# Attention weights of the dilated groups: sent through DRAM as rows and loaded back spread over features, with the score and value runs put side by side

## The chip, the cores and the metric

The kernel runs on one core of a Trainium2 chip. The metric is the device time of one execution in microseconds (us). TensorE (PE) multiplies matrices into eight PSUM banks, VectorE (DVE), ScalarE (ACT) and GpSimd (POOL) work elementwise on SBUF and PSUM, SyncE (SP) and also ACT and POOL issue DMA transfers. Each engine works through its own instructions in order and waits on semaphores for the others.

## The reference, cut to what matters

Two layers of a decoder trunk on x of 512 tokens and 1024 features, all float32. Of each layer, the part that the change touches is the dilated attention: 18 heads of 64 features in three groups of six, with (window, dilation) = (128,1), (512,4), (2048,16). For each head position the three groups' outputs are averaged with weights that are a softmax over the groups' log denominators:

```python
for gi, (window, dilation) in enumerate(ATTN_GROUPS):
    o, lse = _dilated_window_attention(q_a[:, :, gi], k_a[:, :, gi], v_a[:, :, gi], ..., window, dilation)
    outs.append(o.astype(jnp.float32))
    lses.append(lse)
wts = jax.nn.softmax(jnp.stack(lses, axis=0), axis=0)
y_a = jnp.sum(wts[..., None] * jnp.stack(outs, axis=0), axis=0)
...
y_r = _retention(q_r, k_r, v_r)                      # 4 heads, rotary, chunkwise
merged = sigmoid(gate_a) * (y_a @ w_attn_proj) + sigmoid(gate_b) * ((silu(g_r) * y_r) @ w_ret_proj)
x = layer_norm(ALPHA * x + merged @ w_out)
x = layer_norm(ALPHA * x + swiglu(x))
```

## The kernel before, in words

Most of the time goes into large projections. A float32 product is made of three matmuls of 32-bit parts, high by high, high by low and low by high (`mm3`, `whi`/`wlo`, `xh`/`xl`, and `xs` for sums of blocks); the weights are loaded by SP and split by ACT (L347) and DVE (L355). All matmuls are issued by `mm` at L96; rows of the profile tell them apart by their tiles: `ps<-...` are projections, `px<-qk` attention scores, `px<-s,v` attention values.

Attention runs beside the projections as a list of small steps. The steps stand in the queue `side`; after each projection step `tick` takes from it at a rate that `pace` sets, so the places of the steps in the list, with `nothing` as filler, set the order on every engine:

```python
def tick(us):
    if side:
        credit[0] += rate[0] * us
        while side and credit[0] >= 1.0:
            credit[0] -= 1.0
            side.popleft()()
```

Per layer there are three pairs of heads (hp 0, 1, 2). Pairs 0 and 1 run beside other query, key and value projections, pair 2 beside the first rotary projection of the retention part. For one pair and each of four tiles i of 128 queries there are three steps. `scores(i)` issues the products of queries and keys into two PSUM tiles; DVE adds the bias and finds the minimum of the negated scores (L542), ACT takes the exponentials with their sums (L545). `turn(i)` transposes the eight (six for tile 0) blocks on PE (L555) and ACT copies them back (L556). `values(i)` multiplies by the values, and ACT copies the result to `y` (L569). The first group is in token order ("order 0"), the two dilated groups share an order by stride ("order 1"), so two weights per token and head are needed.

After the tiles comes the tail. `swap` stores minima and sums of order 1 to DRAM (`exd`, L583), `swapped` loads them in the other order (`mb`, L586), `weigh` makes both weights per token and head on DVE (L592 to L603) and stores those of order 1 to DRAM (`exd2`, L602; the profile shows it as exd too), `weighed` loads them in stride order (`fa`, L608). For each order, `expand` spreads a weight over the 64 features of its head on POOL (`fe`, L615), `turn_weights` transposes four blocks on PE (L621) into PSUM, and `combine` multiplies `y` by them on DVE (L626, L628) and adds order 1 to order 0 (L630). The tail of one pair runs in the list of the next one; the last tail runs beside the rotary projection and the first retention head. ACT issues the stores and loads of the tail in its own queue.

Of the kernel before, what the change touches and what calls it, by code (L numbers as in the profile page):

```python
# [20 lines left out]
P = 128  # L21
# [35 lines left out]
def hybrid_kernel(ctx, tc, x, x_t, w_first, rel_t, b_cols, b_rows, w_in, w_attn_proj, w_ret_proj, w_out,  # L57
# [457 lines left out]

    latest = {}

    def attention_pair(hp, qk, v, yp, bias, yaT):


        y = yp()
        nm = sm.tile([P, 2, NI, 2], F32, tag="nm", name="nm", bufs=2)
        ls = sm.tile([P, 2, NI, 2], F32, tag="ls", name="ls", bufs=2)
        wrk = {}

        def scores(i):
            tk = slice(i * P, (i + 1) * P)
            pxs = [psum() for _ in range(2)]
            j0 = 1 if i == 0 else 0
            prs = [slice(hh * HD, (hh + 1) * HD) for hh in range(2)]  # L530
            for px, pr in zip(pxs, prs):
                mm(px[:, j0 * P:2 * P], qk[0][pr, 0, tk], qk[0][pr, 1, (i - 1 + j0) * P:(i + 1) * P], True, True)
            for j in range(2):
                for px, pr in zip(pxs, prs):
                    mm(px[:, (2 + j) * P:(3 + j) * P], qk[1 + j][pr, 0, tk], qk[1 + j][pr, 1, tk], True, True)
            ss = [wk.tile([P, 2, 2 * P], F32, tag="w2", name="s") for _ in range(2)]
            for hh in range(2):
                for od in range(2):
                    n0 = j0 * P if od == 0 else 0
                    s = ss[od]  # L540
                    m_, l_ = nm[:, od, i, hh:hh + 1], ls[:, od, i, hh:hh + 1]
                    dve.tensor_tensor_reduce(out=s[:, hh, n0:], in0=pxs[hh][:, od * 2 * P + n0:(od + 1) * 2 * P],  # L542
                                             in1=bias[hp][hh][:, od, n0:], scale=-1.0, scalar=3e38,
                                             op0=ALU.add, op1=ALU.min, accum_out=m_)
                    act.activation(out=s[:, hh, n0:], in_=s[:, hh, n0:], func=AF.Exp, bias=m_, scale=-1.0, accum_out=l_)  # L545
            wrk[i] = (pxs, ss, j0)

        def turn(i):
            pxs, ss, j0 = wrk[i]
            for od in range(2):  # L550
                j1 = j0 if od == 0 else 0
                px = pxs[od].rearrange("p (h c) -> p h c", h=2)
                for hh in range(2):
                    for j in range(j1, 2):
                        pe.transpose(px[:, hh, j * P:(j + 1) * P], ss[od][:, hh, j * P:(j + 1) * P], ident)  # L555
                act.copy(out=ss[od][:, :, j1 * P:], in_=px[:, :, j1 * P:])  # L556
            latest["sT"] = ss[1]

        def values(i):
            pxs, sTs, j0 = wrk.pop(i)  # L560
            px = pxs[0]
            for od in range(2):
                j1 = j0 if od == 0 else 0
                vs = (v[i - 1][:, 0] if i else None, v[i][:, 0]) if od == 0 else (v[i][:, 1], v[i][:, 2])
                for j in range(j1, 2):
                    for hh in range(2):
                        cs = slice(hh * HD, (hh + 1) * HD)
                        mm(px[cs, od * P:(od + 1) * P], vs[j][:, cs], sTs[od][:, hh, j * P:(j + 1) * P], j == j1, j == 1)
            act.copy(out=y[:, :, i], in_=px[:, :2 * P].rearrange("p (o t) -> p o t", o=2))  # L569

        fa = sm.tile([P, 2, NI, 2], F32, tag="fa", name="fa", bufs=2)
        mb = sm.tile([P, NI, 4], F32, tag="mb", name="mb", bufs=2)
        wb = sm.tile([P, NI, 2], F32, tag="wb", name="wb", bufs=2)

        exd = drp.tile([S, 4], F32, tag="exd", name="exd", bufs=2)
        exd2 = drp.tile([S, 2], F32, tag="exd2", name="exd2", bufs=2)

        def swap():

            pk = sm.tile([P, NI, 4], F32, tag="pk", name="pk", bufs=2)  # L580
            act.copy(out=pk[:, :, 0:2], in_=nm[:, 1])
            act.copy(out=pk[:, :, 2:4], in_=ls[:, 1])
            act.dma_start(exd.rearrange("(l r) c -> l r c", r=4), pk)  # L583

        def swapped():
            act.dma_start(mb, exd.rearrange("(i p) c -> p i c", p=P))  # L586

        def weigh():
            mn = sm.tile([P, NI, 2], F32, tag="mn", name="mn", bufs=2)
            ea = sm.tile([P, 2, NI, 2], F32, tag="ea", name="ea", bufs=2)  # L590
            wa = sm.tile([P, NI, 2], F32, tag="wa", name="wa", bufs=2)
            dve.tensor_copy(mn, latest["sT"][:, 0, P:P + 2 * NI].rearrange("p (i h) -> p i h", i=NI))  # L592
            dve.tensor_tensor(out=mn, in0=nm[:, 0], in1=mb[:, :, 0:2], op=ALU.min)
            dve.tensor_tensor(out=ea[:, 0], in0=mn, in1=nm[:, 0], op=ALU.subtract)
            dve.tensor_tensor(out=ea[:, 1], in0=mn, in1=mb[:, :, 0:2], op=ALU.subtract)
            act.activation(out=ea, in_=ea, func=AF.Exp)
            dve.tensor_tensor(out=wa, in0=ea[:, 0], in1=ls[:, 0], op=ALU.mult)
            dve.tensor_tensor(out=wb, in0=ea[:, 1], in1=mb[:, :, 2:4], op=ALU.mult)
            dve.tensor_tensor(out=wa, in0=wa, in1=wb, op=ALU.add)
            dve.reciprocal(out=wa, in_=wa)  # L600
            dve.tensor_tensor(out=wb, in0=ea[:, 1], in1=wa, op=ALU.mult)
            act.dma_start(exd2.rearrange("(i p) c -> p i c", p=P), wb)  # L602
            dve.tensor_tensor(out=fa[:, 0], in0=ea[:, 0], in1=wa, op=ALU.mult)  # L603

        def weighed():

            act.copy(out=fa[:, 1], in_=latest["sT"][:, 0, P:P + 2 * NI].rearrange("p (i h) -> p i h", i=NI))
            act.dma_start(fa[:, 1], exd2.rearrange("(l r) c -> l r c", r=4))  # L608

        wide_, weights = {}, {}  # L610

        def expand(od):

            wide_[od] = work("fe")
            pool.tensor_copy(out=wide_[od].rearrange("p (i h e) -> p i h e", i=NI, h=2),  # L615
                             in_=fa[:, od].unsqueeze(3).to_broadcast([P, NI, 2, HD]))

        def turn_weights(od):
            px = weights[od] = psum()
            for i in range(NI):  # L620
                pe.transpose(px[:, i * P:(i + 1) * P], wide_[od][:, i * P:(i + 1) * P], ident)  # L621

        def combine(od):
            yo = y[:, od].rearrange("p i t -> p (i t)")
            if od == 0:
                dve.tensor_tensor(out=yaT[:, hp], in0=yo, in1=weights[od], op=ALU.mult)  # L626
            else:
                dve.tensor_tensor(out=yo, in0=yo, in1=weights[od], op=ALU.mult)  # L628
                yr = yaT[:, hp].rearrange("p (l r) -> p r l", r=4)
                dve.tensor_tensor(out=yr, in0=yr, in1=y[:, od], op=ALU.add)  # L630

        places = [[] for _ in range(30)]
        for i in range(NI):
            for at, f in ((0, scores), (6, turn), (9, values)):
                places[(0, 7, 14, 20)[i] + at].append(lambda f=f, i=i: f(i))
        ops = [f for p_ in places for f in p_ or [nothing]]
        ops.append(swap)
        steps = [[lambda f=f, od=od: f(od) for f in (expand, turn_weights, combine)] for od in range(2)]
        tail = [swapped, weigh] + steps[0] + [weighed] + steps[1]
        return ops, tail  # L640

    VB = 288
# [10 lines left out]
    def layer(ly, cp):  # L653
# [12 lines left out]
        csp = yap  # L666
        cos = csp.tile([P, S], F32, name="cos")
        sin = csp.tile([P, S], F32, name="sin")

        def slot(name="op", dt=F32R):  # L670
            return opp.tile([P, 2, S], dt, tag="op", name=name)
# [62 lines left out]
        with stage("attn") as ap_, stage("attw", 4) as aw:  # L734
# [212 lines left out]
            for hp in range(HPG // 2):  # L947
# [9 lines left out]
                    qk_slot(2, 2)  # L957
                    qk_put(2, 2, 0, wstat(us, 0))
                drain()
                ops, t_ = attention_pair(hp, [qk[hp, g] for g in range(NG)], load_v(hp), outputs_last if hp == HPG // 2 - 1 else outputs_, bias, yaT)  # L960
                if hp + 1 < HPG // 2:
                    ops.insert(17, lambda hp=hp: load_bias(hp + 1))
                if hp == 0:
# [2 lines left out]
                            pool.tensor_copy(out=tab[:, :1], in_=qk[0, 0][:, 0, :1])  # L966
                    pool.dma_start(cos, c_cos)
                    pool.dma_start(sin, c_sin)
                for at, f in zip((31, 30, 28, 22, 20, 18, 13, 12, 3), reversed(tail)):
                    ops.insert(at, f)  # L970
                side.extend([nothing] * (3, 3, 8)[hp] + ops)
                tail = t_
                pace(25 if hp < 2 else 32)
            n = [nothing]
            side.extend(n * 3 + tail[:1] + n * 8 + tail[1:3] + n * 2 + tail[3:4] + n * 2 + tail[4:5] + n + tail[5:6])
            pace(42)
            rotary(0)
            vg = ret_values_gates(0)
# [4 lines left out]
        with ret:  # L983
# [58 lines left out]
            for h in range(RH):  # L1042
# [8 lines left out]
                if h:  # L1051
                    side.extend([nothing] + ops)
                else:
                    side.extend([nothing] + ops + tail[6:7] + [nothing] * 2 + tail[7:8] + [nothing] + tail[8:] + [nothing])
                pace(15 if h == 0 else 32)
                run(vg)
                drain()
# [556 lines left out]
```

## Time and profile before

| | us |
|---|---|
| median of three runs | 2082.29 (2081.85 to 2082.34) |
| the profiled execution | 2082.44 |
| its span in the trace | 2080.7 |
| PE busy in it | 2066.6 |
| DVE, ACT, POOL busy | 1652.9, 1149.5, 243.4 |

The granted TensorE clock was 0.999 of full speed. The rows that the prediction shows are of five kinds. A group row gives line, engine, operation, tiles as out<-in and count, then the busy time, the mean ns of one, and the idle time before. A row that begins with a time is one of the timeline: start in us from the start of the span, duration, engine, line. A row with an arrow names a wait: who waited, at what line, for which engine's result, then the time in us, the count and the longest. A row with two times and a colon is a stretch: the busy time and the count of PE, PE's weight loads, DVE, ACT and POOL in turn, then the granted clock, the share of the DMA engines and GB/s. A DMA row gives the issuing queue, the KB of each transfer, first and last issue time, and under it the time from issue to landing as smallest, median and largest.

### The profile page before, as it was taken

The numbers are of one execution on the slowest core, as the hardware profiler recorded it, in microseconds if no ns is written. First come the engines' busy times: TensorE is split into PE (matmuls) and PEld (weight loads), VectorE is DVE, ScalarE is ACT, GpSimd is POOL, SyncE is SP. The second block draws the span as 40 slices with busy tenths as digits, with TensorE's granted clock in tenths as the row PEclk, the third lists the DMA queues.
The fourth block names the chain that finished last, engine by engine and source line by source line (L and its number), as shares of the span: only waits on it lengthen the run. The fifth ranks groups of instructions, "written<-read, shape, count | busy, mean of one in ns | idle before, by whom it ended". The sixth has DMA issues, their size and how long they took to land.

```text
span 2080.7 us, 33536 instructions
## 1 busy us (share of the span) xinstructions
PE 2066.6 (99%) x13090; PEld 1849.6 (89%) x13090; DVE 1652.9 (79%) x2343; ACT 1149.5 (55%) x1746; POOL 243.4 (12%) x228
## 2 busy tenths in 40 slices
PE   9999999999999999999999999999999999999998
PEld 9989888888888898989899898888888889989897
DVE  7757888786987798887777578887869877988876
ACT  6577655565563465555355675555655534655551
POOL 1001111100021101011020011111100211110101
PEclk9999999999999999999999999999999999999999
DMA  7856466765679268767358555758656783786871
GB/s 236 217 135 149 122 167 173 192 177 173 207 172 276 63 168 199 190 176 199 94 162 229 139 127 141 178 143 216 172 184 197 173 257 72 182 206 159 203 191 42
DMA packets 275759, 356.92 MB, mean 172 GB/s; under 512 B 21776, under 2 KB 182672, under 8 KB 275600
## 3 DMA queue, kind: packets, MB, share of 16 engines
q1 hardware_dynamic: 199776, 249.08, 38.3%
q0 software_dynamic: 60416, 92.81, 25.0%
q10 hardware_dynamic: 15408, 12.89, 1.9%
q8 instruction: 102, 1.67, 0.3%
q14 instruction: 57, 0.47, 0.1%
HBM read 333.16 MB, written 21.57 MB: 170 GB/s over the span
## 4 chain that ended last, share of the span: by engine, by line
PE 92%; issue 4%; DMA 2%; DVE 1%; ACT 1%; POOL 0%; POOLq 0%; SPq 0%; DVEq 0%; ACTq 0%
PE ps L96 83%; PE px L96 6%; DMA raw<-in_w_in 1%; PE px L555 1%; PE px L1031 1%; PE px L208 0%; PE px L1244 0%; POOL ry L150 0%; DMA xc<-in_x_t 0%; PE px L621 0%; ACT whi L347 0%; DVE xtok L1341 0%; ACT s L545 0%; DMA raw<-in_w_ffn_gate 0%; DVE wlo L355 0%
## 5 line engine op out<-in xcount | busy, mean ns | idle before, releaser
L355 DVE TENSOR_TENSOR wlo<-raw,whi 128x1024 fp32r<-128x1024 f32 (+1 forms) x518 | 601.7, 1171 | 184.0 <-ACT whi L347 167.3
L347 ACT CAST whi<-raw 128x1024 fp32r<-128x1024 f32 (+1 forms) x518 | 516.7, 1008 | 387.6 <-PE ps L96 147.6
L96 PE MATMUL ps<-xs,whi 128*128 128x256 f32 x2176 | 399.2, 284 | 0.4 <-ACT sn L783 0.4
L96 PE MATMUL ps<-whi,xs 128*128 128x512 f32 (+1 forms) x1152 | 347.7, 372 | 0.4 <-ACT whi L347 0.3
L96 PEld LDWEIGHTS ps<-xs,whi 128*128 128x128 f32 x2176 | 339.5, 192 | 4.7 <-issue 1.7
L96 PE MATMUL ps<-xh,whi 128*128 128x256 f32 (+1 forms) x1104 | 318.3, 290 | 0.7 <-ACT xh L107 0.7
L96 PE MATMUL ps<-xl,whi 128*128 128x256 f32 (+1 forms) x1104 | 315.5, 287 | 0.2 <-DVE xl L108 0.2
L96 PE MATMUL ps<-xh,wlo 128*128 128x256 f32 (+1 forms) x1104 | 314.8, 286 | 0.0
L96 PE MATMUL ps<-xs,wlo 128*128 128x256 f32 x1088 | 307.7, 283 | 0.0
L96 PEld LDWEIGHTS ps<-whi,xs 128*128 128x128 f32 x1152 | 209.9, 188 | 35.0 <-ACT whi L347 0.9
L96 PEld LDWEIGHTS ps<-xh,whi 128*128 128x128 f32 x1104 | 210.7, 192 | 7.9 <-issue 1.7
L96 PEld LDWEIGHTS ps<-xl,whi 128*128 128x128 f32 x1104 | 211.5, 192 | 3.0 <-DVE xl L108 1.0
L96 PE MATMUL ps<-wlo,xs 128*128 128x512 f32 (+1 forms) x576 | 213.2, 370 | 0.8 <-DVE wlo L355 0.8
L96 PEld LDWEIGHTS ps<-xh,wlo 128*128 128x128 f32 x1104 | 211.1, 191 | 1.4
L96 PEld LDWEIGHTS ps<-xs,wlo 128*128 128x128 f32 x1088 | 208.5, 192 | 0.0
L96 PE MATMUL ps<-whi,xh 128*128 128x512 f32 (+1 forms) x512 | 193.2, 377 | 0.0
L96 PE MATMUL ps<-wlo,xh 128*128 128x512 f32 (+1 forms) x512 | 190.7, 372 | 0.0
L96 PE MATMUL ps<-whi,xl 128*128 128x512 f32 (+1 forms) x512 | 190.5, 372 | 0.0
L378 DVE TENSOR_TENSOR raw<-raw 128x1024 f32<-128x1024 f32 (+1 forms) x148 | 171.5, 1168 | 0.8
L96 PE MATMUL ps<-whi,ht 128*128 128x512 f32 x544 | 170.1, 391 | 0.0
L338 POOL DMA_DIRECT2D raw<-in_w_in x72 | 86.8, 1219 | 625.8 <-DMA raw<-in_w_in 151.9
L107 ACT CAST whi<-raw 128x1024 fp32r<-128x1024 f32 (+1 forms) x100 | 100.1, 1016 | 83.8 <-PE ps L96 69.4
(226 smaller groups left out, 3225.3 us busy)
## 6 DMA issues: line engine op xcount, KB each, us to landing
raw<-in_w_in SPq DMA_DIRECT2D x164, 512.0 KB, 5.1
raw<-in_w_ffn_up SPq DMA_DIRECT2D x64, 512.0 KB, 5.1
raw<-in_w_in POOLq DMA_DIRECT2D x56, 512.0 KB, 8.2
raw<-in_w_ffn_down SPq DMA_DIRECT2D x52, 512.0 KB, 4.7
raw<-in_w_ffn_gate SPq DMA_DIRECT2D x44, 512.0 KB, 5.2
raw<-in_w_ffn_gate POOLq DMA_DIRECT2D x40, 512.0 KB, 6.9
raw<-in_w_in SPq DMA_DIRECT2D x48, 256.0 KB, 4.9
raw<-in_w_ret_proj SPq DMA_DIRECT2D x24, 512.0 KB, 5.8
```

The costliest lines, as they stand in the source:

```text
L96: pe.matmul(ps, lhsT=a, rhs=b, start=start, stop=stop, skip_group_check=True)
L107: c = act.copy(out=hi, in_=src)
L338: pool.dma_start(r, self.src({"P1": "B12", "P3": "B22"}[n], u), accum_op=ALU.add)
L347: c = act.copy(out=h, in_=src)
L355: dve.tensor_tensor(out=l, in0=src, in1=h.bitcast(F32), op=ALU.subtract)
L378: dve.tensor_tensor(out=r, in0=r, in1=self.t["B22" if n == "P2" else "B21", u], op=ALU.add)
L555: pe.transpose(px[:, hh, j * P:(j + 1) * P], ss[od][:, hh, j * P:(j + 1) * P], ident)
L1031: pe.transpose(px[:, t * P:(t + 1) * P], ys[i][:, t * P:(t + 1) * P], ident)
```

## The change

The weights no longer go over POOL and four transposes. `weigh` writes both orders' weights into one tile `wt` of 16 columns (order, head, tile). The new step `rows_out` transposes it once on PE (L607), ACT copies the 16 rows to `wr` (L609) and stores them to DRAM (L610): 16 rows of 128 weights. `spread(od)` loads the rows of one order back, each head's 512 weights to 64 partitions (two loads of 128 KB, L617), into a tile `fe` that all pairs share; a small ACT copy (L614) ahead of the loads keeps their place in ACT's order. `combine` reads `fe` from SBUF, in the second order with a stride of four. The order of the steps changes too: `both(i)` issues values(i) and right behind it scores(i+1), with four fillers and the turn between; and the steps of the tail move to other places in the next list. The diff:

```diff
@@ -515,7 +515,7 @@
 
     latest = {}
 
-    def attention_pair(hp, qk, v, yp, bias, yaT):
+    def attention_pair(hp, qk, v, yp, bias, yaT, fe):
 
 
         y = yp()
@@ -568,12 +568,12 @@
                         mm(px[cs, od * P:(od + 1) * P], vs[j][:, cs], sTs[od][:, hh, j * P:(j + 1) * P], j == j1, j == 1)
             act.copy(out=y[:, :, i], in_=px[:, :2 * P].rearrange("p (o t) -> p o t", o=2))
 
-        fa = sm.tile([P, 2, NI, 2], F32, tag="fa", name="fa", bufs=2)
+        wt = sm.tile([P, 2, 2, NI], F32, tag="fa", name="wt", bufs=2)
         mb = sm.tile([P, NI, 4], F32, tag="mb", name="mb", bufs=2)
         wb = sm.tile([P, NI, 2], F32, tag="wb", name="wb", bufs=2)
 
         exd = drp.tile([S, 4], F32, tag="exd", name="exd", bufs=2)
-        exd2 = drp.tile([S, 2], F32, tag="exd2", name="exd2", bufs=2)
+        exd2 = drp.tile([4 * NI, P], F32, tag="exd2", name="exd2", bufs=2)
 
         def swap():
 
@@ -598,45 +598,42 @@
             dve.tensor_tensor(out=wb, in0=ea[:, 1], in1=mb[:, :, 2:4], op=ALU.mult)
             dve.tensor_tensor(out=wa, in0=wa, in1=wb, op=ALU.add)
             dve.reciprocal(out=wa, in_=wa)
-            dve.tensor_tensor(out=wb, in0=ea[:, 1], in1=wa, op=ALU.mult)
-            act.dma_start(exd2.rearrange("(i p) c -> p i c", p=P), wb)
-            dve.tensor_tensor(out=fa[:, 0], in0=ea[:, 0], in1=wa, op=ALU.mult)
-
-        def weighed():
-
-            act.copy(out=fa[:, 1], in_=latest["sT"][:, 0, P:P + 2 * NI].rearrange("p (i h) -> p i h", i=NI))
-            act.dma_start(fa[:, 1], exd2.rearrange("(l r) c -> l r c", r=4))
-
-        wide_, weights = {}, {}
-
-        def expand(od):
-
-            wide_[od] = work("fe")
-            pool.tensor_copy(out=wide_[od].rearrange("p (i h e) -> p i h e", i=NI, h=2),
-                             in_=fa[:, od].unsqueeze(3).to_broadcast([P, NI, 2, HD]))
-
-        def turn_weights(od):
-            px = weights[od] = psum()
-            for i in range(NI):
-                pe.transpose(px[:, i * P:(i + 1) * P], wide_[od][:, i * P:(i + 1) * P], ident)
+            for od in range(2):
+                dve.tensor_tensor(out=wt[:, od].rearrange("p h i -> p i h"), in0=ea[:, od], in1=wa, op=ALU.mult)
+
+        def rows_out():
+            n = 4 * NI
+            px = psum()
+            pe.transpose(px[:n, :P], wt.rearrange("p o h i -> p (o h i)"), ident)
+            r = sm.tile([P, P], F32, tag="wr", name="wr", bufs=1)
+            act.copy(out=r[:n], in_=px[:n, :P])
+            act.dma_start(exd2, r[:n])
+
+        def spread(od):
+
+            act.copy(out=fe[:, :2 * NI], in_=latest["sT"][:, 0, P:P + 2 * NI])
+            for h in range(2):
+                q = (2 * od + h) * NI
+                act.dma_start(fe[h * HD:(h + 1) * HD], exd2[q:q + NI].rearrange("i p -> (i p)").partition_broadcast(HD))
 
         def combine(od):
-            yo = y[:, od].rearrange("p i t -> p (i t)")
             if od == 0:
-                dve.tensor_tensor(out=yaT[:, hp], in0=yo, in1=weights[od], op=ALU.mult)
+                dve.tensor_tensor(out=yaT[:, hp], in0=y[:, od].rearrange("p i t -> p (i t)"), in1=fe, op=ALU.mult)
             else:
-                dve.tensor_tensor(out=yo, in0=yo, in1=weights[od], op=ALU.mult)
+                dve.tensor_tensor(out=y[:, od], in0=y[:, od], in1=fe.rearrange("p (l r) -> p r l", r=4), op=ALU.mult)
                 yr = yaT[:, hp].rearrange("p (l r) -> p r l", r=4)
                 dve.tensor_tensor(out=yr, in0=yr, in1=y[:, od], op=ALU.add)
 
-        places = [[] for _ in range(30)]
+        def both(i):
+            values(i)
+            if i + 1 < NI:
+                scores(i + 1)
+
+        ops = [lambda: scores(0)]
         for i in range(NI):
-            for at, f in ((0, scores), (6, turn), (9, values)):
-                places[(0, 7, 14, 20)[i] + at].append(lambda f=f, i=i: f(i))
-        ops = [f for p_ in places for f in p_ or [nothing]]
+            ops += [nothing] * 4 + [lambda i=i: turn(i)] + [nothing] * 2 + [lambda i=i: both(i)]
         ops.append(swap)
-        steps = [[lambda f=f, od=od: f(od) for f in (expand, turn_weights, combine)] for od in range(2)]
-        tail = [swapped, weigh] + steps[0] + [weighed] + steps[1]
+        tail = [swapped, weigh, rows_out] + [lambda f=f, od=od: f(od) for od in range(2) for f in (spread, combine)]
         return ops, tail
 
     VB = 288
@@ -666,6 +663,7 @@
         csp = yap
         cos = csp.tile([P, S], F32, name="cos")
         sin = csp.tile([P, S], F32, name="sin")
+        fe = yap.tile([P, S], F32, name="fe")
 
         def slot(name="op", dt=F32R):
             return opp.tile([P, 2, S], dt, tag="op", name=name)
@@ -957,7 +955,7 @@
                     qk_slot(2, 2)
                     qk_put(2, 2, 0, wstat(us, 0))
                 drain()
-                ops, t_ = attention_pair(hp, [qk[hp, g] for g in range(NG)], load_v(hp), outputs_last if hp == HPG // 2 - 1 else outputs_, bias, yaT)
+                ops, t_ = attention_pair(hp, [qk[hp, g] for g in range(NG)], load_v(hp), outputs_last if hp == HPG // 2 - 1 else outputs_, bias, yaT, fe)
                 if hp + 1 < HPG // 2:
                     ops.insert(17, lambda hp=hp: load_bias(hp + 1))
                 if hp == 0:
@@ -966,13 +964,13 @@
                             pool.tensor_copy(out=tab[:, :1], in_=qk[0, 0][:, 0, :1])
                     pool.dma_start(cos, c_cos)
                     pool.dma_start(sin, c_sin)
-                for at, f in zip((31, 30, 28, 22, 20, 18, 13, 12, 3), reversed(tail)):
+                for at, f in zip((33, 27, 26, 19, 14, 11, 3), reversed(tail)):
                     ops.insert(at, f)
                 side.extend([nothing] * (3, 3, 8)[hp] + ops)
                 tail = t_
                 pace(25 if hp < 2 else 32)
             n = [nothing]
-            side.extend(n * 3 + tail[:1] + n * 8 + tail[1:3] + n * 2 + tail[3:4] + n * 2 + tail[4:5] + n + tail[5:6])
+            side.extend(n * 3 + tail[:1] + n * 8 + tail[1:2] + n * 2 + tail[2:3] + n * 4 + tail[3:4] + n * 6 + tail[4:6])
             pace(42)
             rotary(0)
             vg = ret_values_gates(0)
@@ -1051,7 +1049,7 @@
                 if h:
                     side.extend([nothing] + ops)
                 else:
-                    side.extend([nothing] + ops + tail[6:7] + [nothing] * 2 + tail[7:8] + [nothing] + tail[8:] + [nothing])
+                    side.extend([nothing] + ops + tail[6:] + [nothing])
                 pace(15 if h == 0 else 32)
                 run(vg)
                 drain()
```

The order of instructions on TensorE in pair 0 of layer 0, before (-) and now (+): `ps<-` are the projections beside it, `s,v` values(0) and `qk` scores(1).

```order
 L96 MATMUL ps<-xs,wlo 128x256
+L96 MATMUL px<-s,v 64x128 x6
 L96 MATMUL px<-qk 128x256 x2
 L96 MATMUL px<-qk 128x128 x4
@@ -681,11 +684,4 @@
 L96 MATMUL ps<-xs,whi 128x256 x2
 L96 MATMUL ps<-xs,wlo 128x256
-L96 MATMUL px<-s,v 64x128 x6
```

The values run stood by itself between projections behind the scores run, and now stands directly ahead of it.

The order on ScalarE in pair 2 of layer 0, before, from the exponentials of tile 1 to the copy of turned scores (`wb` is the weight of order 1):

```order
L545 ACTIVATE s,ls<-s,nm 128x256 x2
L347 CAST whi<-raw 128x1024
L602 DMA exd_1680<-wb 128x4x2
L545 ACTIVATE s,ls<-s,nm 128x256 x2
L347 CAST whi<-raw 128x1024
L556 COPY s<-px 128x512
```

And now, from the copy of the turned weights to the exponentials of tile 2:

```order
L609 COPY wr<-px 16x128
L614 COPY fe<-s 128x8
L347 CAST whi<-raw 128x1024
L107 CAST rot<-sn 128x2x256
L610 DMA exd_1681<-wr 16x128
L569 COPY y<-px 128x2x128
L617 DMA fe<-exd_1681 64x512
L107 CAST rot<-sn 128x2x256
L545 ACTIVATE s,ls<-s,nm 128x256 x2
L617 DMA fe<-exd_1681 64x512
L545 ACTIVATE s,ls<-s,nm 128x256 x2
```

The store of the weights was followed by exponentials alone, its load came a tile later; now a store and both loads of order 0 stand among the copies and exponentials of one tile.

The order on VectorE in the same place, before (L542 are the minima of tile 2, `rs`, `sn` and `rot` rotary work):

```order
L542 ISA s,nm<-px,bias 128x256
L542 ISA nm 128x1
L678 TENSOR_TENSOR rs<-sn,sin 128x512
L626 TENSOR_TENSOR yaT<-y,px 128x512
L679 TENSOR_TENSOR sn<-sn,cos 128x512
L355 TENSOR_TENSOR wlo<-raw,whi 128x1024
```

And now:

```order
L542 ISA s,nm<-px,bias 128x256
L542 ISA nm 128x1
L708 TENSOR_TENSOR sn<-ps,sn 128x512
L676 TENSOR_TENSOR rs<-sn,sin 128x512
L677 TENSOR_TENSOR sn<-sn,cos 128x512
L621 TENSOR_TENSOR yaT<-y,fe 128x512
L678 TENSOR_TENSOR sn<-sn,rs 128x256
```

The product of order 0 keeps about its place behind tile 2's minima; what it reads was a transpose in PSUM and is now the loaded tile `fe`.

## The prediction

> **What bounds the kernel now.** I read the page first (span, part 1, part 4), then TensorE's waits, then TensorE's timeline around one run of each kind, then the chain from scores to turned scores, then the transfers that go through DRAM. The page:
>
> ```profile
> span 2080.7 us, 33536 instructions
> ...
> PE 2066.6 (99%) x13090; PEld 1849.6 (89%) x13090; DVE 1652.9 (79%) x2343; ACT 1149.5 (55%) x1746; POOL 243.4 (12%) x228
> ...
> PE 92%; issue 4%; DMA 2%; DVE 1%; ACT 1%; POOL 0%; POOLq 0%; SPq 0%; DVEq 0%; ACTq 0%
> ```
>
> TensorE (PE) is busy for 99% of the span and carries 92% of the chain that ended last. Its waits are eight rows that sum to 5.0 us; first and last:
>
> ```profile
> PE px L96 <- DVE warm L800: 1.5, 1, 1.5
> ...
> PE ps L96 <- DVE xl L108: 0.2, 1, 0.2
> ```
>
> So a microsecond taken from PE is a microsecond of the time, and one of new waiting on PE is lost. The change does both, and the sum is made from PE's side. The profiled execution took 2082.44 us (span 2080.7 and 1.7 around it), 0.15 above the median of the runs, 2082.29.
>
> **Part 1: PE work removed, 12 runs of four transposes (L621).**
>
> ```profile
> L621 PE MATMUL px<-ident,fe 128*128 128x128 f32 x48 | 7.2, 272 | 0.0
> 157.08 0.28 PE L96 MATMUL ps<-xs,whi 128*128 128x256 f32 x1
> 157.20 0.28 PE L96 MATMUL ps<-xs,wlo 128*128 128x256 f32 x1
> ...
> 157.56 0.28 PE L96 MATMUL ps<-xs,wlo 128*128 128x256 f32 x1
> 157.68 0.60 PE L621 MATMUL px<-ident,fe 128*128 128x128 f32 x4
> 158.03 0.48 PE L96 MATMUL ps<-xs,whi 128*128 128x256 f32 x2
> 158.35 0.28 PE L96 MATMUL ps<-xs,wlo 128*128 128x256 f32 x1
> ```
>
> Busy time counts overlapping ends, so I take starts. Projection matmuls of 256 columns start 0.12 apart. After the one at 157.56 the third next would start at 157.92; with the run between it starts at 158.35. A run costs 0.43, twelve cost **5.2 us**: -5.2.
>
> **Part 2: PE work added, six transposes of the 16-row weight tile.** No row has one. Such a transpose uses a 128x32 part of the array, so the nearest rows are the runs on other array shapes, values (128*64) and scores (64*128):
>
> ```profile
> 109.63 0.28 PE L96 MATMUL ps<-xs,wlo 128*128 128x256 f32 x1
> 109.84 0.88 PE L96 MATMUL px<-s,v 128*64 128x128 f32 x12
> 110.65 0.51 PE L96 MATMUL ps<-xs,whi 128*128 128x256 f32 x2
> 110.99 0.29 PE L96 MATMUL ps<-xs,wlo 128*128 128x256 f32 x1
> ...
> 170.59 0.60 PE L621 MATMUL px<-ident,fe 128*128 128x128 f32 x4
> 171.12 0.43 PE L96 MATMUL px<-s,v 128*64 128x128 f32 x2
> ```
>
> From 109.63 the third projection matmul comes at 110.99 instead of 109.99: a values run of six costs 1.00. Six times 0.11 is work (a transpose of the same 128 columns starts 0.11 after another: 0.43 for four), so 0.34 is the visit to another shape: the step in (0.21 for 0.12) and the late steps after it. One added transpose costs between 0.1 (no visit) and 0.45 (visit and work); I take 0.35, near the visits: **+2.1** (ends 0.6 and 2.7).
>
> **Part 3: values next to scores.** In TensorE's order (the first place shown with the change) the values run (s,v) moved up against the next scores run (qk). Over both layers the order has 52 separate visits before and 30 after: 18 merges, and 4 runs that were cut in two are whole. A merge leaves one direct change of shape. No row has values to scores; the nearest is 170.59 to 171.12: the fourth transpose starts 0.33 into its run, at 170.92, and values 0.20 later instead of 0.11, so 0.09 for one change. A merge then saves 0.34 - 0.10 = 0.24, 18 save 4.3 (ends: 0.10 each if the change costs nearly a visit, 1.8; the whole visit, 6.1), the four cuts 1.4: **-5.7**. The Trainium skill, "TensorEngine Tiling (Array Packing)", Key Properties, says that a change of tiling mode drains the array. That agrees with 0.21 for 0.12 here, and by it values to scores, two different modes, must drain as well; if that drain cost a visit, part 3 would be -3.2 and the forecast 2.5 us higher.
>
> PE's own work: -5.2 + 2.1 - 5.7 = **-8.8** (ends -5.7 and -12.1).
>
> **Part 4: turns move nearer to their scores.** A turn of tile i needs the minimum on VectorE (DVE, L542) and the exponentials on ScalarE (ACT, L545). In pair 2, beside the first rotary projection, tiles 2 and 3:
>
> ```profile
> 197.13 1.15 PE L96 MATMUL px<-qk 64*128 64x256 f32 x12
> 203.13 0.51 ACT L545 ACTIVATE s<-s,nm 128x256 f32<-128x256 f32 x1
> 205.15 1.03 PE L555 MATMUL px<-ident,s 128*128 128x128 f32 x8
> 206.81 1.15 PE L96 MATMUL px<-qk 64*128 64x256 f32 x12
> 208.22 0.39 PE L96 MATMUL ps<-wlo,xh 128*128 128x512 f32 x1
> 208.45 0.40 PE L96 MATMUL ps<-whi,xl 128*128 128x512 f32 x1
> 212.57 0.51 ACT L545 ACTIVATE s<-s,nm 128x256 f32<-128x256 f32 x1
> 213.62 1.04 PE L555 MATMUL px<-ident,s 128*128 128x128 f32 x8
> ```
>
> The last exponential ends 5.4 us after scores(2) (203.64 - 198.28) and 5.1 after scores(3) (213.08 - 207.96); the turns came 6.9 and 5.7 after. The new order has 27 projection matmuls of 256 columns between scores(2) and its turn, 27 x 0.12 + 0.2 = 3.4, and 16 of 512 columns (0.23 each) for scores(3), 3.7. If the chains stayed, PE would wait 2.0 and 1.4. But the first four transposes need only earlier exponentials, and DVE's new order has less rotary work ahead of tile 2's minima. I take 2.0 per layer: **+4** (ends 0 and 8: 3.4 per layer and some tenths in pairs 0 and 1).
>
> **Part 5: weights through DRAM.** In ScalarE's order in the same place (the second place shown with the change) the load of fe (L617) waits in ACT's queue for the store (L610) to land, with tile 2's exponentials behind it. In VectorE's order (the third place) the product that reads fe (L621, formerly L626 with a PSUM operand) stands right behind scores(2)'s minima; behind it are rotary work, two splits of weights and tile 3's minima, for which turn(3) waits.
>
> ```profile
> L583 ACTq DMA_DIRECT2D exd<-pk x6: 326/338/338, 130.4 to 1249.2; - x6
> DMA to landing us min/median/max: 1.4/1.5/5.6
> L602 ACTq DMA_DIRECT2D exd<-wb x6: 372/377/377, 151.3 to 1263.9; - x6
> DMA to landing us min/median/max: 4.1/4.4/8.0
> L934 SPq DMA_DIRECT2D v<-v_d x24: 319/338/1325, 58.0 to 1202.5; - x24
> DMA to landing us min/median/max: 1.8/2.7/5.8
> 190.00:195.00 5.00, 5.00 (x48) 4.70 (x47) 4.88 (x18) 4.00 (x11) 1.18 (x1) 1.00 1.11 255
> 206.00:212.00 6.00, 6.00 (x46) 4.45 (x44) 6.00 (x16) 3.74 (x10) 0.72 (x1) 1.00 0.01 1
> 203.51 0.68 DVE L626 TENSOR_TENSOR yaT<-y,px 128x512 f32<-128x512 f32 x1
> L347 ACT CAST whi<-raw 128x1024 fp32r<-128x1024 f32 x44 | 45.5, 1046 | 29.3 <-PE ps L96 18.9 <-issue 5.6 <-DVE yb L1021 2.5
> ```
>
> From the turned weights on: copies and casts ahead of the store 2.3, its landing e, the load's landing f. DVE reaches L621 after 15 projection matmuls (1.8), values and scores (2.1), the minima and a cast (2.3) and three products (2.0): 8.2. The product is late by e + f - 5.9. Stores into DRAM landed in 1.4 to 8.0 us, 128 KB loads (as each half of fe is) in 1.8 to 5.8. In 190 to 195 the DMA engines are full (share 1.11), so both lie in their upper halves: I take 4.5 and 4.4, 3.0 late per layer, all of it passed on, since DVE is full there (4.88 of 5.00, then 6.00 of 6.00): **+6** (ends 0, and 15.8 for 8.0 + 5.8). In pairs 0 and 1 of the tail DVE has slack and I count nothing. The Trainium skill, "DMA: Bandwidth & Descriptors", Anatomy of one DMA, gives about 2.0 us of fixed cost per transfer; an estimate by it, 4.0 for store and load, would make part 5 zero. The rows agree with it only where the engines are idle.
>
> At nothing: POOL's twelve copies go (POOL 12% busy; PE's waits name no transfer), ACT's six copies, six more order-keeping copies and 18 more DMA issues lie in its idle time outside that place (3.74 of 6.00 busy), the product of the second order reads fe strided on DVE, some 0.4 more at most, six times, where DVE waits for others.
>
> **Sum.** -8.8 + 4 + 6 = +1.2: 2082.44 + 1.2, **2083.6 us**.
>
> **Rivals.** Quiet landings (e + f under 5.9): part 5 is zero, -4.8, 2077.6. For it: the load of 128 KB landed in 2.7 by the median; against it the full DMA engines. No waits at all: DVE's new order also spares the turns, -8.8, 2073.6; against it chains of 5.1 and 5.4 for distances of 3.4 and 3.7. Late loads, slower than before: store and load land as the slowest rows did, part 5 is 15.8, 2082.44 - 8.8 + 4 + 15.8 = 2093.4; it decides from e + f = 10.4 in pair 2 (part 5 over 9). For it: the store at this place landed in 8.0 before; against it, that store had 8-byte pieces and the new one has 512-byte rows. That the merges don't happen is excluded by the order.
>
> **How the numbers follow.** 0.2% is 4.2 us, about what a measurement here tells from no change. Forecast, within that: 0.44, of its own 2078.3 to 2086.6. Quiet landings 0.20, three in four of them past 0.2% faster. No waits 0.08. Late loads 0.28. Faster 0.15 + 0.08 = 0.23, same 0.44 + 0.05 = 0.49, slower 0.28. The range 2076.5 to 2093 leaves out most of "no waits" and the worst of the late loads.
>
> **What would show it.** Right: no L621 transposes, values to scores 0.2 apart, PE waits at turns of tiles 2 and 3 in pair 2 of a microsecond or more, DVE idle before yaT<-y,fe there. Wrong: PE's waits still near 5 us (then 2074 to 2078), a landing of fe above 6 us (then 2090 and more), or an added transpose far over 0.45.

## The result, and the profile after

The changed kernel took 2105.1 us (median of 4 runs, 2103.6 to 2108.24) against 2082.32 for the kernel before; the ratio is 1.0112 (1.01 to 1.0124). It is 22.8 us slower, outside the predicted range. The profiled execution took 2103.6 us. Its page:

```profile
span 2101.8 us, 33434 instructions
...
PE 2069.3 (98%) x13048; PEld 1851.7 (88%) x13048; DVE 1654.7 (79%) x2343; ACT 1149.2 (55%) x1758; POOL 231.8 (11%) x216
...
PE 86%; DMA 4%; issue 4%; DVE 2%; ACT 1%; POOL 0%; ACTq 0%; SPq 0%; POOLq 0%; DVEq 0%
PE ps L96 79%; PE px L96 5%; DMA fe<-exd 2%; DMA raw<-in_w_in 1%; DMA exd<-wr 1%; DVE wlo L355 1%; PE px L555 1%; PE px L1029 1%; ACT whi L347 0%; PE px L208 0%; ACT s L545 0%; PE px L1242 0%; POOL ry L150 0%; DMA raw<-in_w_ffn_gate 0%; DMA raw<-in_w_first 0%
```

The span grew by 21.1 us, and PE's share of the last chain fell from 92% to 86%. The store `exd<-wr` and the loads `fe<-exd` are now on that chain. PE's waits, longest in total first (us, times, longest):

```profile
PE px L555 <- ACT s L545: 6.0, 6, 2.6
PE ps L96 <- DVE sn L504: 5.2, 2, 2.6
PE ps L96 <- ACT sn L781: 4.7, 2, 2.8
PE ps L96 <- DVE sn L789: 2.8, 2, 1.8
```

These four were 0.4 us together and are 18.7. They have three places. Pair 1 of layer 0 first, on ACT, where a row with ACTq is the issue of a transfer:

```profile
154.69 0.34 ACTq L610 DMA_DIRECT2D exd<-wr  x1
...
157.56 1.15 ACTq L617 DMA_DIRECT2D fe<-exd  x2
158.76 0.51 ACT L545 ACTIVATE s<-s,nm 128x256 f32<-128x256 f32 x1 [3.32 <-issue]
...
160.74 0.56 ACT L781 COPY sn<-ps 128x512 f32<-128x512 f32 x1
```

The load cannot be issued until the store has landed (154.69 to 157.50). ACT idles 3.32 us, and behind the load stand four exponentials and the eviction L781, which PE waits for. On DVE:

```profile
161.39 0.69 DVE L621 TENSOR_TENSOR yaT<-y,fe 128x512 f32<-128x512 f32 x1 [4.25 <-ACT sn L781]
...
170.30 1.14 DVE L623 TENSOR_TENSOR y<-y,fe 128x512 f32<-128x512 f32 x1 [1.46 <-DMA fe<-exd]
...
172.45 0.69 DVE L789 TENSOR_TENSOR sn<-sn,ps 128x512 f32<-128x512 f32 x1
```

The product idles 4.25 us. The profile names L781, which ended then too; the second load landed at 161.26. The second product waits for its own load, and L789 behind it releases PE's next projection. PE's rows:

```profile
161.35 0.51 PE L96 MATMUL ps<-xs,whi 128*128 128x256 f32 x2 [1.93 <-ACT sn L781]
173.19 0.39 PE L96 MATMUL ps<-xh,whi 128*128 128x256 f32 x1 [1.80 <-DVE sn L789]
```

Pair 2, the place of the prediction, on ACT and then on DVE (the last ACT row is of layer 1):

```profile
199.13 0.33 ACTq L610 DMA_DIRECT2D exd<-wr  x1
204.63 0.46 ACTq L617 DMA_DIRECT2D fe<-exd  x1
205.14 0.62 ACT L107 CAST rot<-sn 128x512 fp32r<-128x512 f32 x1 [3.75 <-DMA exd<-wr]
...
1251.97 0.62 ACT L107 CAST rot<-sn 128x512 fp32r<-128x512 f32 x1 [5.55 <-DMA exd<-wr]
```

```profile
211.31 0.69 DVE L621 TENSOR_TENSOR yaT<-y,fe 128x512 f32<-128x512 f32 x1 [2.09 <-DMA fe<-exd]
```

The store landed after 5.44 us and the load after 6.43: e + f is 11.9. In layer 1 they took 7.22 and 3.80, DVE did not idle before the product, and PE stood before the turn of tile 2, whose exponentials follow the held load on ACT:

```profile
1253.14 0.69 PE L555 MATMUL px<-ident,s 128*128 128x128 f32 x2 [2.65 <-ACT s L545]
```

The last tail, beside the first retention head, has the longest wait for a landing:

```profile
250.81 1.09 DVE L623 TENSOR_TENSOR y<-y,fe 128x512 f32<-128x512 f32 x1 [4.24 <-DMA fe<-exd]
```

Behind it on DVE is L504, for which PE waited 2.6 us in each layer. Over the kernel, from the answer on the tile `fe`:

```profile
L617 ACTq DMA_DIRECT2D fe<-exd x24: 452/465/620, 157.6 to 1289.6; - x24
...
  DMA fe<-exd: 17.5, 6
...
DMA to landing us min/median/max: 2.8/3.5/7.1
```

DVE idled 17.5 us for landings of `fe`.

The waits are not all of the loss. Stretches of 3.413 us (columns: PE, PE's loads, DVE, ACT, POOL busy, granted clock, DMA share, GB/s), two by two:

```profile
170.47:173.89 3.42, 1.62 (x14) 1.39 (x13) 3.39 (x4) 2.24 (x5) 0.00 (x0) 1.00 0.07 26
173.89:177.30 3.41, 3.41 (x19) 3.41 (x18) 2.27 (x3) 1.97 (x3) 0.00 (x0) 0.50 0.06 10
204.60:208.02 3.42, 1.80 (x15) 1.29 (x13) 2.20 (x7) 2.77 (x10) 0.00 (x0) 1.00 1.12 256
208.02:211.43 3.41, 3.41 (x14) 3.07 (x13) 1.29 (x3) 2.30 (x4) 0.00 (x0) 0.50 0.44 134
252.39:255.80 3.41, 2.04 (x13) 1.65 (x11) 3.41 (x6) 1.03 (x2) 0.00 (x0) 1.00 0.68 107
255.80:259.21 3.41, 2.19 (x10) 1.84 (x11) 3.41 (x8) 2.31 (x4) 0.00 (x0) 1.00 0.55 154
```

In the first two pairs PE idled 1.80 and 1.62 us of a stretch, and in the next one its clock was half. In the third, a gap of 2.59 us fell on both stretches, 1.37 and 1.21, and the clock stayed. The changed kernel has six half-clock stretches outside its ends, two from pair 1, three from pair 2 and one from the last tail over the two layers; the one before has none. They take 9.7 us of PE's time. The account of the span: 18.5 more of PE idle (22.2 instead of 3.7, all gaps between PE's rows counted), 9.7 of half clock, and PE's busy time without that loss is 6.9 shorter (2059.7 instead of 2066.6): +21.3; the ends of the span, outside PE's rows, are 0.1 shorter.

### The profile page after: what moved, and what is told of

It is laid out like the page before. It is cut to its first block, busy times and chain, and to the rows that moved or that the text cites. A ratio compares the mean times of both kernels' runs of the same rounds, so it can differ in the third digit from the quotient of the medians.

```text
span 2101.8 us, 33434 instructions
## 1 busy us (share of the span) xinstructions
PE 2069.3 (98%) x13048; PEld 1851.7 (88%) x13048; DVE 1654.7 (79%) x2343; ACT 1149.2 (55%) x1758; POOL 231.8 (11%) x216
## 4 chain that ended last, share of the span: by engine, by line
PE 86%; DMA 4%; issue 4%; DVE 2%; ACT 1%; POOL 0%; ACTq 0%; SPq 0%; POOLq 0%; DVEq 0%
PE ps L96 79%; PE px L96 5%; DMA fe<-exd 2%; DMA raw<-in_w_in 1%; DMA exd<-wr 1%; DVE wlo L355 1%; PE px L555 1%; PE px L1029 1%; ACT whi L347 0%; PE px L208 0%; ACT s L545 0%; PE px L1242 0%; POOL ry L150 0%; DMA raw<-in_w_ffn_gate 0%; DMA raw<-in_w_first 0%
```

## The experiments

### The order alone, and the rows alone

`order_alone` takes the new order of steps and keeps the old weights:

```diff
-        places = [[] for _ in range(30)]
...
+        def both(i):
+            values(i)
+            if i + 1 < NI:
+                scores(i + 1)
...
-                for at, f in zip((31, 30, 28, 22, 20, 18, 13, 12, 3), reversed(tail)):
+                for at, f in zip((33, 32, 30, 23, 21, 19, 14, 12, 3), reversed(tail)):
```

> The new order of steps (values and the next scores side by side, turns nearer) with the old way of the weights (POOL spreading, four transposes per order). Theory 'loads': the changed kernel lost its time to the store and the loads of the weights, which hold ACT's queue and VectorE's product; without them the order gives its 5.7 us of merged runs less up to 3 us of waits at turns: 2077 to 2081, clock 0.999. Rival 'order': turns that stand too near to their scores stall TensorE (the trace of the changed kernel puts 6.0 us of waits at the turns) and start the rest: above 2090.

2078.77 us (11 runs) against 2082.12; ratio 0.9982 (0.9973 to 0.9991), as theory "loads" had it. In its trace PE waits 0.2 us at the turns.

`rows_alone` is the reverse: the changed kernel with the old `places`, the tail at (31, 25, 24, 18, 13, 10, 3).

> The old order of steps (values apart from scores) with the weights as rows through DRAM, the tail's steps at the same share of the list as in the changed kernel. Theory 'loads': the waits come with it, 2095 to 2108, clock under 0.997. Rival 'order': 48 transposes fewer and no harm, 2079 to 2083.

2096.87 us; ratio 1.0073 (1.006 to 1.0087), in the range of theory "loads" again. The loss came with the rows and the gain with the order, so the rival "order" as the only cause is out. But the two do not add: +14.8 and -3.4 make 11.4, and together they are +22.8. What the rows cost with the old order is in these waits:

```profile
PE ps L96 <- DVE sn L786: 5.1, 2, 2.7
PE ps L96 <- DVE sn L504: 4.8, 2, 2.5
PE px L555 <- ACT s L545: 1.7, 2, 0.8
```

They are the evictions behind the products. The turns cost 1.7 instead of 6.0, and the eviction that stood behind ACT's held load in pair 1 (L781, here L778) 0.4 instead of 4.7: there the store had landed at 153.93, before the load's turn came at 155.70. So half of the loss came only where the rows stand with the new order and its places.

### No loads

```diff
         fe = yap.tile([P, S], F32, name="fe")
+        pool.memset(fe, 0.5)
...
-                act.dma_start(fe[h * HD:(h + 1) * HD], exd2[q:q + NI]...partition_broadcast(HD))
```

> The changed kernel without the loads of the rows (fe is filled once per layer with a constant; the store stays), so the weights don't enter the result. Theory 'loads': waits of TensorE under 8 us, clock 0.999, 2073 to 2080. Rival 'order': waits at the turns stay, above 2088.

2076.14 us; ratio 0.997 (0.9959 to 0.9982). Without its loads the changed kernel is 6 us faster than the old one: the loads cost 29.0 us (2105.1 - 2076.1). That is not the waits alone, since DVE's order differs too: in pair 2 the first product stands at 193.57, ahead of tile 2's minima, and not at 211.31 behind them. What is left at the turns:

```profile
L555 PE MATMUL px<-ident,s 128*128 128x128 f32 x180 | 26.2, 277 | 1.7 <-ACT s L545 1.0 <-DVE nm L542 0.8
```

The old order of steps without the loads, with fe a constant likewise:

> The old order of steps with the weights as rows, without the loads (fe is a constant, the weights don't enter the result): TensorE has 48 transposes fewer and six small ones more, and waits for nothing new. If the terms of the sum add up: 2082.3 - 3.1 = 2079.2, 2078 to 2080.5. If the waits of that version had another source than the loads: above 2085.

2081.80 us, ratio 0.9998 (0.9989 to 1.0007): a miss by 2.6. PE's busy time is 2062.2, 4.4 below the old kernel. But with nothing to wait for, the second product of pair 1 (L623, L625) stands ahead of tile 3's minima, at 164.06; in `rows_alone`, with the same places in the list, it stands behind them, and in the old kernel it starts at 172.46. The eviction L787 behind it came late and PE waited 1.4 us in each layer.

### Which wait: ACT's queue or the product

`act_held` keeps every store and load and lets the products read a ready tile:

```diff
-... in1=fe, op=ALU.mult)
+... in1=cos, op=ALU.mult)
-... in1=fe.rearrange("p (l r) -> p r l", r=4), op=ALU.mult)
+... in1=cos.rearrange("p (l r) -> p r l", r=4), op=ALU.mult)
```

> The changed kernel with VectorE's two products per pair reading a tile that is ready (the cosine table) instead of the loaded rows; store, loads and their places on ACT stay, the weights don't enter the result. ACT's queue is still held by the load that waits for the store, VectorE waits for no landing. Theory 'both waits pay': of the 18 us of new waits some 10.7 hang on ACT's held queue (the turns and the eviction L781) and 8 on the products: 2083 to 2092. Rival 'the queue alone': 2096 or more. Rival 'the products alone': 2075 to 2080.

2092.21 us; ratio 1.0043 (1.0029 to 1.0057): 0.2 above the range of "both waits pay" and below its rival's 2096. The products also moved: with the ready tile the first one stands at 137.01 in pair 1 and 180.13 in pair 2, ahead of the store and the loads, instead of at 161.39 and 211.31. `input_rows` lets the loads read an input instead of the stored weights, so ACT is not held:

```diff
-exd2[q:q + NI].rearrange("i p -> (i p)").partition_broadcast(HD)
+c_cos[q].partition_broadcast(HD)
```

> The changed kernel with the loads reading rows of an input table in DRAM (same sizes, same places) instead of the stored weights, so no load waits for the store, and ACT's queue isn't held; VectorE's products still wait for the landing. The weights don't enter the result. Theory 'both waits pay': 2080 to 2092. Rival 'the queue alone': 2075 to 2080. Rival 'the products alone': 2096 or more.

2089.56 us; ratio 1.003 (1.0018 to 1.0042), within "both waits pay". Both keep about half of the 29 us: 16.1 and 13.4 above `no_loads`. What PE waits for tells them apart, in `act_held` first:

```profile
PE px L555 <- ACT s L545: 6.5, 6, 3.4
PE ps L96 <- ACT sn L781: 5.7, 2, 3.0
```

These are the turns and the eviction behind ACT's held load; no wait for L789 or L504 is left. In `input_rows` the first product idles for the landing (its row: busy, mean ns, idle before and who ended it), and PE waits, besides 4.3 at turns, for the eviction behind the second product:

```profile
L621 DVE TENSOR_TENSOR yaT<-y,fe 128x512 f32<-128x512 f32 x6 | 4.1, 690 | 13.1 <-DMA fe<-const_cos 13.1
```

```profile
PE ps L96 <- DVE sn L789: 4.8, 2, 2.7
```

Here no wait for L781 is left. So each wait alone stops PE, by another path: ACT's hold by L781 and the turns, the products by the evictions behind them.

The store, the loads and the small copy on POOL's queue:

```diff
-            act.dma_start(exd2, r[:n])
+            pool.dma_start(exd2, r[:n])
-            act.copy(out=fe[:, :2 * NI], ...
+            pool.tensor_copy(out=fe[:, :2 * NI], ...
-                act.dma_start(fe[h * HD:...
+                pool.dma_start(fe[h * HD:...
```

> The changed kernel with the store, the two loads per order and the small copy ahead of them on POOL instead of ACT, so ACT's exponentials and evictions no longer stand behind a load that waits for the store; VectorE's product still waits for the landing. If the held ACT queue is the larger part: TensorE's waits fall by half or more, 2080 to 2092. If VectorE's wait for the landing is the larger part: 2098 or more.

2126.68 us; ratio 1.0208 (1.0192 to 1.0224), the slowest of all. As a test of ACT's hold it is inconclusive, since it moved the landings as well: the store of pair 2 was issued at 202.15 and took 9.01 us, and the loads went out at 211.71.

```profile
DVE yaT L621 <- DMA fe<-exd: 36.8, 6, 6.5
```

PE's waits for turns, L504 and L789 came to 14.6, 10.6 and 8.6, and none for L781 is left. So with ACT's queue free and landings this late, waits that start at the products can cost more than the whole change.

### Loads together, and further apart

Order 0's rows now go straight into the output tile and the product overwrites them, so both orders can be loaded at once; in `two_far` and `two_late` the last tail's steps are set apart likewise:

```diff
-        tail = [...] + [lambda f=f, od=od: f(od) for od in range(2) for f in (spread, combine)]
+            to = yaT[:, hp] if od == 0 else fe
+        tail = [...] + [lambda f=f, od=od: f(od) for f in (spread, combine) for od in range(2)]
-zip((33, 27, 26, 19, 14, 11, 3), reversed(tail))
+zip((33, 26, 19, 19, 14, 11, 3), reversed(tail))
+zip((33, 31, 19, 19, 9, 7, 2), reversed(tail))
+zip((34, 29, 18, 18, 11, 6, 2), reversed(tail))
```

The three places are those of `two_buf`, `two_far` and `two_late`.

> The changed kernel with the rows of order 0 loaded into the output tile yaT, which the product then overwrites in place, and order 1 into fe: both loads are issued together at the place of the first, the products stay at their places. The second product no longer waits for a load that could start only behind the first product. Theory: its waits go (8 us of waits and two or three half-clock windows), the hold of ACT and the first product's wait stay: 2085 to 2097. Rival, four loads together land later and the first product waits longer: 2100 or more.

2101.03 us; ratio 1.0083 (1.0068 to 1.0098): the rival. The second product's wait is down to 0.9, and the first's is 22.1 us over the kernel.

> As the one before, but the steps are set apart: the turned weights are stored ten steps ahead of the loads, the loads twelve and fourteen steps ahead of the products (some 6 to 9 us each). Theory 'loads': nothing waits any more, and the kernel has the whole of the saved TensorE work: 2074 to 2079, below the old one. Rival: landings past 8 us beside full DMA engines, or the products now late for what follows: 2084 or more.

2087.22 us; ratio 1.0023 (1.0014 to 1.0032). No half-clock stretch is left, but the rival's range holds it: turns still wait (PE's waits), and the first product idles 11.8 us over the kernel.

```profile
PE px L555 <- ACT s L545: 4.1, 7, 0.9
```

> As the version with the loads set far ahead, with the products later (order 0 behind tile 3's scores, order 1 at the end of the list) and the transpose of the weights later behind the weights' arithmetic. Before, VectorE's second product and its addition (2.2 us together) stood ahead of tile 3's minima in pair 2, and TensorE waited for the weights' arithmetic. Theory 'placing': the remaining waits at turns go, 2076 to 2080. Rival 'VectorE is full, whatever the place': 2083 to 2088.

2093.24 us; ratio 1.0052 (1.004 to 1.0065): slower than both forecasts. In pair 2 the two loads of order 0, issued from 197.07 on, took 7.07 and 8.92 us, and on DVE:

```profile
206.63 0.69 DVE L622 TENSOR_TENSOR yaT<-y,yaT 128x512 f32<-128x512 f32 x1 [4.24 <-DMA yaT<-exd]
```

DVE did nothing for 4.24 us. Behind the product stood the rotary sums, behind these ACT's cast of `rot`, behind that the copies of the turned scores, and behind these the values: PE waited 4.6 us for them, although the product's own result is needed by nobody there.

The only version with the full result that beats both kernels is `order_alone`, 3.4 us (0.18%) below the old one, with an interval that lies wholly below 1.

## Why the prediction was wrong, point by point

**Part 1, right.** The runs of four transposes are gone; one costs 0.44 where it stands between 256-column projections in the old kernel, and 0.45 to 0.46 between 512-column ones. Twelve are -5.3, for -5.2.

**Part 2, at its low end.** The added transpose pays no visit:

```profile
151.37 0.28 PE L96 MATMUL ps<-xs,wlo 128*128 128x256 f32 x1
151.48 0.27 PE L607 MATMUL px<-ident,wt 128*16 128x128 f32 x1
...
151.83 0.28 PE L96 MATMUL ps<-xs,wlo 128*128 128x256 f32 x1
```

From 151.37 the third projection comes at 151.83 instead of 151.73: 0.1, four times; twice, between 512-column projections in the last tail, it is 0.2. Six cost +0.8, not +2.1. The nearest rows, visits to 64 rows or columns, were the wrong kin.

**Part 3, right in sum, by two errors that offset each other.** A merged run of the changed kernel, and the scores alone before:

```profile
107.14 0.28 PE L96 MATMUL ps<-xs,wlo 128*128 128x256 f32 x1
107.35 0.94 PE L96 MATMUL px<-s,v 128*64 128x128 f32 x12
108.22 1.15 PE L96 MATMUL px<-qk 64*128 64x256 f32 x12
...
109.64 0.27 PE L96 MATMUL ps<-xs,wlo 128*128 128x256 f32 x1
```

```profile
115.10 0.28 PE L96 MATMUL ps<-xs,wlo 128*128 128x256 f32 x1
115.31 1.15 PE L96 MATMUL px<-qk 64*128 64x256 f32 x12
...
116.73 0.28 PE L96 MATMUL ps<-xs,wlo 128*128 128x256 f32 x1
```

Scores alone cost 116.73 - 115.10 - 0.36 = 1.27, values alone 1.00 (as the prediction read), merged 2.07 at the median of six such runs (this one 2.14): a merge saves 0.19 by unrounded starts, not 0.24, and 18 save 3.4 for 4.3. The four cuts were worth 0.40 and 0.55 each, some 1.9 for 1.4. Together -5.3, for -5.7. The direct change between values and scores so costs 0.34 - 0.19 = 0.15, not 0.10 and far from a visit's 0.34. The Trainium skill, "TensorEngine Tiling (Array Packing)", Key Properties, says that a change of tiling mode drains the array. The trace agrees that values to scores is not free: the scores start 0.21 after the last values (108.02 to 108.23) where 0.11 is the step within the run; of the two prices that the prediction weighed for it, the low one was nearer. PE's own work sums to -5.3 + 0.8 - 5.3 = -9.8, for -8.8.

**Part 4, right in size.** Summed over `no_loads`, the transposes of turns start 4.0 us later in all than at the old kernel's pace (1.3 at the first ones, 2.7 within the runs), for +4, though in the DVE order of that version. With the -9.8 that is -5.8, and the span of `no_loads` is 6.3 below the old one. `order_alone` has 1.7 of it, and -5.3 + 1.7 = -3.6 is near its -3.4.

**Part 5, the step that failed.** +6 was forecast and 29.0 measured. Three things were missed. First, the places: "In pairs 0 and 1 of the tail DVE has slack and I count nothing", and the last tail has no term at all. DVE's slack is no help to what stands in order behind the product: the evictions L789 and L504 that PE waits for are behind it, and L781 is behind ACT's held load. By the gaps and half-clock stretches of the trace, pair 1 cost 7.5 (L781 and L789) + 3.4 and the last tail 5.2 (L504) + 1.7.

Second, pair 2, the one place with a price. The landings were mis-sized: e + f was 11.9 in layer 0 and 11.0 in layer 1, not 8.9, past the 10.4 from which the rival "late loads" decides. The 4.0 estimated from the Trainium skill, "DMA: Bandwidth & Descriptors", Anatomy of one DMA, was a third of the 11.9; that section describes transfers issued by POOL, and ACT issues these. And the wait was mostly another one. The price was put on the late product, which idled 2.1 us in layer 0 and not at all in layer 1. PE's gaps there, 5.9 over both layers (those of part 4 among them), are all waits of turns for exponentials: 4.8 at tile 2, whose exponentials stand behind the held load on ACT, and 1.1 at tile 3. The prediction named that hold and gave it no price.

Third, no term had the clock: pair 2's gaps brought 5.1 more, and 9.7 came in all. The profiled execution's span is 27.4 above that of `no_loads` (2101.8 - 2074.4): 17.4 more of PE's gaps, 9.7 of half clock and 0.4 of other PE time. The rival's direction was right, and so was the sign "a landing of fe above 6 us (then 2090 and more)"; but its 15.8 was made for the late product in one place of three.

The old kernel's rows had a hint. Its loads `fa<-exd` landed after up to 5.1 us too, but POOL's copies read them. The answer on the tile `fa`:

```profile
its engine sat idle before it (us, times) until:
  DVE fa L603: 60.7, 4
...
who waited for it (us, times):
  POOL fe L615: 60.7, 4
...
DMA to landing us min/median/max: 1.5/3.4/5.1
```

POOL idled 60.7 us before these copies until DVE had made the first weight, and no wait for the landing itself stands there. Besides, the answer names ACT with 1.0 us and PE's weight loads with 0.3: a late copy there cost next to nothing. In the change the reader of the landed rows is DVE.

## What to carry to other kernels

A transfer through DRAM is cheap when the engine that waits for it has nothing else in its order, and dear when that engine evicts for TensorE: list, for each new wait, every instruction behind it on that engine and follow it to TensorE, even if the result itself is not urgent. An engine that issues a load right behind the store it reads is held for the store's landing, with its compute behind it (ACT idled 3.3 to 5.6 us so here). Take a compound change apart early: here the order of steps was worth -3.4 us by itself, hidden under a loss of 29 by the loads, nearly half of which came only with that order. And look at the order in the trace of each part: a version that leaves out a load can also move what read it.

## What the runs showed of the hardware

In these traces the granted clock changes only on a fixed grid of 3.413 us, whatever the place of a gap: within a trace all its changes lie a whole number of such stretches apart, within 5 ns. Over the twelve traces (old, new and ten experiments), every full-clock stretch outside the ends with 1.61 us or more of PE idle, 23 of them, was followed by a stretch at half clock; none of the next 40, with 0.76 to 1.56 us, was. Half a clock for 3.413 us costs 1.7 us of TensorE's work, as much as the gap itself. In a half-clock stretch less idle kept it there: 1.15 us at 1252.5 in the changed kernel. So a gap of 2.6 us costs 2.6 or 4.3 by where it falls on the grid, which may be part of why the changed kernel's four runs spread over 4.6 us; that was not tested.

Landing times of the same 128 KB load differed with the DMA engines' share: 2.75 us at 215.0 in the changed kernel, where it was 0.22, and 6.43 us at 204.6, where it was 1.12 in the first 3.4 us. That the share is the cause was not tested by itself.
